# Bias tables written head by head, and the first norm's sums taken from rows of the input by ScalarE

## The chip, the cores and the metric

The kernel runs on one NeuronCore of a Trainium2 chip, as one launch. The metric is the device time of that launch in microseconds (us). TensorE's granted clock stands in the profile as a share of its upper level: 1.00 is 2.4 GHz, 0.50 is 1.2 GHz.

## The reference

One decoder layer on x of 512 rows (tokens) and 2048 columns, all in float32. What matters here:

```python
h = rmsnorm(x, norm_pre_g)                     # x * rsqrt(mean(x*x over 2048 columns) + 1e-6) * g
proj = h @ w_in                                # one projection for everything below
# group A: differential attention, 8 heads; logits + T5 relative bias, causal softmax
# group B: 8 heads over a shared latent (ckv); an indexer (iq, ik, iw) picks 128 keys for each query;
#          logits + T5 relative bias
y = concat(o_a * silu(za), o_b * silu(zb)) @ w_out
x = x + rmsnorm(y, norm_post_g)
```

The bias of a head depends only on the distance of query and key, so one row of 512 numbers for each of the 16 heads holds all of it.

## The kernel before

**Projections.** Everything is kept transposed, tokens along the free axis. The input comes twice: `xT`, 16 tiles of 128 columns by 512 tokens, which the products need, and `xn`, the rows, which before were read only at the end for the residual. Each matmul in float32 is split in a high and a low part (`hh`, `hl` of the input, `wh`, `wl` of a weight) and done as three products (`triple`, L162 to L164). The weights come in *units* of up to 128x1024 in the order in which they are used: units 0 to 5 for ckv (`wck`), 6 and 7 for the indexer's keys (`wik`), and from unit 8 on two to a projection of 128 outputs (`wT`): gate, iq, gate, iq and so on. A unit is loaded by SP's queue into `wf` (2 buffers), then split by ScalarE (`wh`, L124) and VectorE (`wl`, L125) into 3 buffers; `use` asks for that some units ahead.

**The first norm's scale.** The projections are made from x times g, without the row scale; the scale comes in when a projection leaves PSUM, as a multiplication by `rB`. Before, GpSimd squared each tile of `xT` (L185) and TensorE summed the squares over the 128 partitions by four products with a column of ones, `ssx` (L195). `rstd` (L203, L204) makes the reciprocal root `rx`, GpSimd lays it on the diagonal of `dg` (L210) and one product with `ones` (L211, `spread`) brings it to all partitions; ScalarE copies it to `rB` (L219). Projections leave PSUM through three `pj` banks, and none can leave before `rB` is there.

**The bias.** A product (L327) makes the bias rows of 16 heads, VectorE copies them (L330), and GpSimd's queue writes them to DRAM (`bd`, L332). `lay_tables` (L341) then writes each row 128 times into a DRAM table, each time one element further, so that a plain read (`strip`, L347, SP's queue) gives the 128x512 tile of biases which a head needs.

**What sets the order.** The code is handed to a scheduler that places the instructions of each engine; each engine, and SP's queue of DMA starts, then takes its own in the order placed. An instruction that waits holds up all behind it on that engine. `strip` has two buffers, and the scheduler has placed the reads for heads 0 and 1 early in SP's queue, among the weight loads.

Of the kernel before, what the change touches and what calls it, by code (L numbers as in the profile page):

```python
# [5 lines left out]
F32 = mybir.dt.float32  # L6
F32R = mybir.dt.float32r
AF = mybir.ActivationFunctionType
OP = mybir.AluOpType
# [4 lines left out]
D = 2048  # L14
KT = 16
# [10 lines left out]
def hybrid_layer(tc, xT, xn, wck, wT, wik, wva, wuv, wo, gpre, gpost, sub, kvg, ikg, lq1, lk1, lq2, lk2, relb, oneh, out):  # L26
    nc = tc.nc
    from contextlib import ExitStack
    with ExitStack() as st:
        S = st.enter_context(tc.tile_pool(name="s", bufs=1))  # L30
        P = st.enter_context(tc.tile_pool(name="p", bufs=1, space=PSUM))
        DR = st.enter_context(tc.tile_pool(name="d", bufs=1, space=DRAM))
# [4 lines left out]
        def lg_bank():  # L37
            return P.tile([128, 512], F32, name="lg", bufs=2)
# [7 lines left out]
        def tmp(name="tq", bufs=2):  # L46
            return S.tile([128, 512], F32, name=name, bufs=bufs)
# [42 lines left out]
        def load_to(n):  # L90
            while pos["load"] < min(n, len(units)):
                i = pos["load"]
                ap, shp = units[i]
                c = shp[0] * shp[1]
                nm, bf = ("wf", 2) if flags["begin"] is not None else ("qk", 4)
                t = S.tile([128, 1024], F32, name=nm, bufs=bf)
                with tc.high_priority(lead()):
                    nc.sync.dma_start(t[:, :c], ap)
                stage[i] = t
                pos["load"] += 1  # L100
# [3 lines left out]
        def split_to(n):  # L104
            while pos["split"] < min(n, len(units)):
                i = pos["split"]
                load_to(i + 1)
                c = units[i][1][0] * units[i][1][1]
                t = stage.pop(i)
                names = [("wh", 3), ("wl", 3)]  # L110
                if i >= len(units) - 8:
                    names = [last.pop(0), last.pop(0)]
                w = []
                for nm, bf in names:
                    if nm == "pt0a":
                        w.append([S.tile([128, 512], F32R, name=x, bufs=1) for x in ("pt0a", "pt0b")])
                    else:
                        a = S.tile([128, 1024], F32R, name=nm, bufs=bf)
                        w.append([a[:, :512], a[:, 512:]] if units[i][1][1] == 512 else [a[:, :c]])
                m = c // len(w[0])  # L120
                with tc.high_priority(lead()):
                    for q in range(len(w[0])):
                        src = t[:, q * m:(q + 1) * m]
                        nc.scalar.copy(w[0][q], src)  # L124
                        nc.vector.tensor_tensor(w[1][q], src, w[0][q].bitcast(F32), op=OP.subtract)  # L125
                ready[i] = w
                pos["split"] += 1

        def use(ahead=3):
            i = pos["use"]  # L130
            pos["use"] += 1
            if ahead:
                load_to(i + ahead + 1)
                split_to(i + ahead)
            nk, n = units[i][1]
            w = ready.pop(i)
            per = nk // len(w[0])
            return [[w[a][k // per][:, (k % per) * n:(k % per + 1) * n] for k in range(nk)] for a in range(2)]
# [11 lines left out]
        onec = S.tile([128, 1], F32, name="onec")  # L150
# [2 lines left out]
        nc.gpsimd.memset(ones, 1.0)  # L153
        ident = S.tile([128, 128], F32, name="ident")
        make_identity(nc, ident)
        ssx = P.tile([128, 4], F32, name="av", bufs=1)
        gp = S.tile([128, KT], F32, name="gp")
        xts, hh, hl, sqx = [], [], [], []
        ckp = [lg_bank(), lg_bank()]

        def triple(ps, a, b, x, y, k):
            nc.tensor.matmul(ps, a, x, start=(k == 0), stop=False)  # L162
            nc.tensor.matmul(ps, a, y, start=False, stop=False)  # L163
            nc.tensor.matmul(ps, b, x, start=False, stop=(k == KT - 1))  # L164

        for n, (ka, kb) in enumerate(CUTS):
            for k in range(ka, kb):
                t = S.tile([128, 512], F32, name=f"go{k}")
                nc.sync.dma_start(t, xT[k])
                xts.append(t)  # L170
                if k == 0:
                    nc.sync.dma_start(gp, gpre)
                    load_to(1)
                if k + 1 < KT and k + 1 == kb - 1:
                    load_to(n + 2)
            for k in range(ka, kb):
                a = S.tile([128, 512], F32R, name=f"hh{k}")
                b = S.tile([128, 512], F32R, name=f"hl{k}")
                nc.scalar.activation(a, xts[k], AF.Copy, scale=gp[:, k:k + 1])
                nc.vector.scalar_tensor_tensor(b, xts[k], gp[:, k:k + 1], a.bitcast(F32),  # L180
                                               op0=OP.mult, op1=OP.subtract)
                hh.append(a)
                hl.append(b)
                sq = S.tile([128, 512], F32, name="tq", bufs=2)
                nc.gpsimd.tensor_tensor(sq, xts[k], xts[k], op=OP.mult)  # L185
                sqx.append(sq)
            split_to(n + 1)
            wh, wl = use(0)
            for k in range(ka, kb):
                for u in range(2):  # L190
                    cs = slice(u * 128, u * 128 + 128)
                    triple(ckp[u], wh[k - ka][:, cs], wl[k - ka][:, cs], hh[k], hl[k], k)
                sq = sqx[k]
                for i in range(4):
                    nc.tensor.matmul(ssx[:, i:i + 1], sq[:, i * 128:(i + 1) * 128], onec,  # L195
                                     start=(k == 0 and i == 0), stop=(k == KT - 1 and i == 3))
        flags["begin"] = tc.cur_priority

        mhalf = S.tile([128, 4], F32, name="mhalf")
# [2 lines left out]
        def rstd(dst, ssq, n):  # L202
            nc.vector.tensor_scalar(dst, ssq, 1.0 / n, EPS, op0=OP.mult, op1=OP.add)  # L203
            nc.gpsimd.tensor_tensor(dst, dst, mhalf[:, :dst.shape[1]], op=OP.pow)  # L204
# [6 lines left out]
            nc.tensor.matmul(bank, ones, dg, start=True, stop=True)  # L211


        rx = S.tile([128, 4], F32, name="rx")
        rstd(rx, ssx, D)
        rB = S.tile([128, 512], F32, name="rB")
        bank = av_bank()
        spread(rx, bank)
# [8 lines left out]
        def proj_T(n0=0, m=128):  # L227
            ps = proj_bank()
            kk = 0
            while kk < KT:  # L230
                wh, wl = use()
                for a, b in zip(wh, wl):
                    triple(ps[:m, n0:], a, b, hh[kk][:, n0:], hl[kk][:, n0:], kk)
                    kk += 1
            return ps

        def pair(name, bufs):
            return S.tile([128, 2, 512], F32R, name=name, bufs=bufs)
# [25 lines left out]
        def scaled(ps, scale, n0=0):  # L264
            t = tmp()
            nc.vector.scalar_tensor_tensor(t[:, n0:], ps[:, n0:], scale, rB[:, n0:], op0=OP.mult, op1=OP.mult)  # L266
            return t
# [4 lines left out]
        for u in range(2):  # L272
            t = S.tile([128, 512], F32, name="e", bufs=2)
# [3 lines left out]
        for u in range(2):  # L277
            sq = tmp()
# [20 lines left out]
        sq = tmp()  # L299
# [31 lines left out]
        bd = DR.tile([16, 640], F32, name="bd")  # L331
# [2 lines left out]


        W = 768
        tables = [DR.tile([2, 128, W], F32, name=f"table{n}") for n in range(8)]

        def lay_tables(n):
            d = tables[n]  # L340
            nc.gpsimd.dma_start(bass.AP(tensor=d.tensor, offset=d.offset, ap=[[128 * W, 2], [W + 1, 128], [1, 640]]),  # L341
                                bass.AP(tensor=bd.tensor, offset=bd.offset + 2 * n * 640,
                                        ap=[[640, 2], [0, 128], [1, 640]]))

        def strip(h):
            g = S.tile([128, 512], F32, name="strip", bufs=2)
            nc.sync.dma_start(g, tables[h // 2][h % 2, :, 127:639])  # L347
            return g


# [16 lines left out]
        def gate():  # L367
            m = len(go)
            ps = proj_T()
            t = tmp()  # L370
            nc.vector.tensor_tensor(t, ps, rB, op=OP.mult)
            g = S.tile([128, 512], F32, name=f"go{m}")
            nc.scalar.activation(g, t, AF.Silu)
            go.append(g)
            if m < 8:
                lay_tables(m)


        def select():
# [17 lines left out]
        for m in range(8):  # L397
            ps = proj_T(n0=128)
            t = scaled(ps, 1.0, 128)
            iq = pair("v", 3)  # L400
            stacked(iq, t, 128)
            for i in range(1, 4):
# [3 lines left out]
                for g in range(2):  # L406
                    h = 2 * m + g
# [155 lines left out]
        for h in range(8):  # L563
# [3 lines left out]
            t = scaled(proj_T(), 0.125)  # L567
            q = pair("qk", 4)
            stacked(q, t)
            t = scaled(proj_T(), 1.0)  # L570
            k = pair("qk", 4)
# [33 lines left out]
        for n in range(4):  # L605
# [30 lines left out]
            for i in range(4):  # L636
# [12 lines left out]
                for a, b in zip(cuts, cuts[1:]):  # L649
                    o = (banks[i] if a == 0 else proj_bank())[:, a:b]  # L650
                    for kp in range(8):
# [3 lines left out]
                        for k in range(2):  # L655
# [5 lines left out]
                                             stop=(kk == 15))  # L661
# [7 lines left out]
                for q in range(4):  # L669
                    if i == 3 and q == 1:  # L670
                        t = S.tile([128, 512], F32, name="sq", bufs=1)
# [72 lines left out]
```

## Time and profile before

| | |
|---|---|
| runs | 1090.49, 1091.66, 1092.74 us; median 1091.66 |
| the profiled execution | 1091.52 us; span 1089.7 us from first to last instruction |
| TensorE busy | 1064.5 us |
| TensorE, mean granted clock | 0.990 |
| VectorE, ScalarE, GpSimd busy | 573.3, 411.9, 90.8 us |
| DMA | 111.97 MB, mean 103 GB/s |

TensorE is busy nearly throughout, so a time saved anywhere else shows only where TensorE waits for it. The span leaves out 1.8 us of the profiled execution's own time.

### The profile page before, as it was taken

The page shows a single profiled execution, that of the slowest core. Times are in us where ns is not written, and L with a number is a line of the kernel's source. Part 1 is how long each engine was busy: PE and PEld are TensorE (multiplying, and loading weights), DVE is VectorE, ACT ScalarE, POOL GpSimd, SP SyncE. Part 2 cuts the span into 40 slices and gives each one's busy share as a digit, 9 for nine tenths or more (in the row PEclk, how much of TensorE's full clock was granted, in tenths as well). Part 3 has the DMA queues.
Part 4 walks back from the last instruction along what each step waited for, and adds up shares of the span by engine and source line. Part 5 has one row for each costly group of instructions (what it writes and reads, how often), then busy time and mean ns, then how long its engine had stood idle before and what let it go on. Part 6 is the DMA issues. An engine that isn't in the chain of part 4 may idle for free.

```text
span 1089.7 us, 14175 instructions
## 1 busy us (share of the span) xinstructions
PE 1064.5 (98%) x5531; PEld 914.8 (84%) x5531; DVE 573.3 (53%) x1143; ACT 411.9 (38%) x773; POOL 90.8 (8%) x110
## 2 busy tenths in 40 slices
PE   8999949999999999999999999999999999999997
PEld 6888848898889889889889888888888888888886
DVE  7225526457993456456456457554545565423353
ACT  6124324333222356356356356332323353323320
POOL 4323300000000001101101100200000000000001
PEclk9999969999999999999999999999999999999999
DMA  8122572222232232222222223222222232333445
GB/s 280 59 93 82 143 210 97 97 97 93 82 100 94 97 97 78 85 90 81 88 84 86 88 71 105 88 86 79 87 68 88 87 97 79 98 108 105 136 134 193
DMA packets 43154, 111.97 MB, mean 103 GB/s; under 512 B 11504, under 2 KB 11632, under 8 KB 43088
## 3 DMA queue, kind: packets, MB, share of 16 engines
q1 hardware_dynamic: 34128, 104.49, 29.3%
q0 software_dynamic: 8960, 6.59, 2.6%
q8 instruction: 43, 0.70, 0.3%
q14 instruction: 23, 0.19, 0.1%
HBM read 106.77 MB, written 9.48 MB: 107 GB/s over the span
## 4 chain that ended last, share of the span: by engine, by line
PE 93%; DMA 4%; issue 2%; SPq 0%; POOL 0%; ACT 0%; DVE 0%; DVEq 0%; ACTq 0%; POOLq 0%
PE pj L162 18%; PE pj L163 18%; PE pj L164 18%; PE pj L461 3%; PE pj L460 3%; PE pj L459 3%; PE lg L544 3%; PE av L442 3%; PE pj L616 2%; PE pj L618 2%; PE pj L617 2%; DMA table<-bd 2%; PE tr L431 2%; PE lg L260 2%; PE lg L262 2%
## 5 line engine op out<-in xcount | busy, mean ns | idle before, releaser
L164 PE MATMUL pj<-hh,wl 128*128 128x512 f32 (+2 forms) x912 | 353.7, 388 | 0.0
L162 PE MATMUL pj<-hh,wh 128*128 128x512 f32 (+2 forms) x912 | 352.2, 386 | 0.1
L163 PE MATMUL pj<-hl,wh 128*128 128x512 f32 (+2 forms) x912 | 351.0, 385 | 0.0
L124 ACT CAST wh<-wf 128x1024 fp32r<-128x1024 f32 (+2 forms) x181 | 164.7, 923 | 428.5 <-PE pj L163 205.2
L125 DVE TENSOR_TENSOR wl<-wf,wh 128x1024 fp32r<-128x1024 f32 (+2 forms) x181 | 191.8, 1071 | 233.7 <-ACT wh L124 230.9
L164 PEld LDWEIGHTS pj<-hh,wl 128*128 128x128 f32 (+1 forms) x912 | 171.3, 188 | 31.8 <-issue 1.8
L162 PEld LDWEIGHTS pj<-hh,wh 128*128 128x128 f32 (+1 forms) x912 | 171.4, 188 | 31.4 <-issue 1.7
L163 PEld LDWEIGHTS pj<-hl,wh 128*128 128x128 f32 (+1 forms) x912 | 171.2, 188 | 30.8 <-issue 0.7
L461 PE MATMUL pj<-wh,hl 128*128 128x256 f32 x256 | 74.4, 291 | 0.0
L459 PE MATMUL pj<-wh,hh 128*128 128x256 f32 x256 | 73.1, 286 | 0.0
L460 PE MATMUL pj<-wl,hh 128*128 128x256 f32 x256 | 72.7, 284 | 0.0
L266 DVE SCALAR_TENSOR_TENSOR tq<-pj,rB 128x512 f32<-128x512 f32 (+1 forms) x40 | 26.6, 664 | 64.3 <-PE pj L164 63.5
L459 PEld LDWEIGHTS pj<-wh,hh 128*128 128x128 f32 x256 | 48.8, 191 | 1.1 <-issue 0.7
L461 PEld LDWEIGHTS pj<-wh,hl 128*128 128x128 f32 x256 | 48.9, 191 | 0.8 <-issue 0.7
L460 PEld LDWEIGHTS pj<-wl,hh 128*128 128x128 f32 x256 | 48.9, 191 | 0.4
L204 POOL TENSOR_TENSOR ro<-ro,mhalf 128x4 f32<-128x4 f32 x8 | 9.6, 1201 | 400.9 <-DVE ro L203 400.9
L544 PE MATMUL lg<-ck,qk 128*128 128x256 f32 (+3 forms) x192 | 38.3, 325 | 0.0
L617 PE MATMUL pj<-wl,hh 128*128 128x512 f32 x96 | 37.5, 391 | 0.0
L616 PE MATMUL pj<-wh,hh 128*128 128x512 f32 x96 | 37.3, 391 | 0.0
L618 PE MATMUL pj<-wh,hl 128*128 128x512 f32 x96 | 37.2, 389 | 0.0
L544 PEld LDWEIGHTS lg<-ck,qk 128*128 128x128 f32 x192 | 31.9, 189 | 3.6 <-issue 0.2
L413 DVE SCALAR_TENSOR_TENSOR sc<-e,iw,sc 128x256 f32<-128x256 f32 (+2 forms) x45 | 27.7, 616 | 10.1 <-ACT e L409 8.0
(349 smaller groups left out, 1514.3 us busy)
## 6 DMA issues: line engine op xcount, KB each, us to landing
wf<-in_wT_dram SPq DMA_DIRECT2D x112, 512.0 KB, 3.5
wf<-in_wo_dram SPq DMA_DIRECT2D x32, 512.0 KB, 3.5
wf<-in_wva_dram SPq DMA_DIRECT2D x16, 512.0 KB, 3.5
table<-bd POOLq DMA_DIRECT2D x8, 640.0 KB, 20.5
go<-in_xT_dram SPq DMA_DIRECT2D x16, 256.0 KB, 6.0
strip<-table SPq DMA_DIRECT2D x16, 256.0 KB, 3.5
out_dram<-go SPq DMA_DIRECT2D x16, 256.0 KB, 3.7
e<-in_xn_dram SPq DMA_DIRECT2D x8, 256.0 KB, 3.4
```

What stands on the lines that cost most here:

```text
L124: nc.scalar.copy(w[0][q], src)
L125: nc.vector.tensor_tensor(w[1][q], src, w[0][q].bitcast(F32), op=OP.subtract)
L162: nc.tensor.matmul(ps, a, x, start=(k == 0), stop=False)
L163: nc.tensor.matmul(ps, a, y, start=False, stop=False)
L164: nc.tensor.matmul(ps, b, x, start=False, stop=(k == KT - 1))
L459: nc.tensor.matmul(o, hh[kk][:, ts], wh[k], start=(kk == 0 and i % 2 == 0), stop=False)
L460: nc.tensor.matmul(o, hh[kk][:, ts], wl[k], start=False, stop=False)
L461: nc.tensor.matmul(o, hl[kk][:, ts], wh[k], start=False, stop=(kk == 15 and i % 2 == 1))
L544: nc.tensor.matmul(bank[:, :w], q[u][:, x, i * 128:(i + 1) * 128], ck[u][:, y, :w], start=(n == 0), stop=(n == 5))
L616: nc.tensor.matmul(banks[i], oh_[kk][:, ts], wh[k], start=(kk == 0), stop=False)
L617: nc.tensor.matmul(banks[i], oh_[kk][:, ts], wl[k], start=False, stop=False)
L618: nc.tensor.matmul(banks[i], ol_[kk][:, ts], wh[k], start=False, stop=(kk == 15))
```

## The change

It touches two things. First, GpSimd's squares and the products with the column of ones are dropped; in their place SP's queue loads the rows of x in eight pieces of 128x1024 into `v` (three buffers), ScalarE squares each and sums along the row, and VectorE adds the two halves. Second, the eight table writes of two heads each, made at the gates, become sixteen of one head each, made where the head's strip is read; the tables get a common name with two buffers.

```diff
-        ssx = P.tile([128, 4], F32, name="av", bufs=1)
...
-                sq = S.tile([128, 512], F32, name="tq", bufs=2)
-                nc.gpsimd.tensor_tensor(sq, xts[k], xts[k], op=OP.mult)
-                sqx.append(sq)
...
-                sq = sqx[k]
-                for i in range(4):
-                    nc.tensor.matmul(ssx[:, i:i + 1], sq[:, i * 128:(i + 1) * 128], onec,
-                                     start=(k == 0 and i == 0), stop=(k == KT - 1 and i == 3))
...
+        ssx = S.tile([128, 8], F32, name="ssx")
+        for i in range(4):
+            for hf in range(2):
+                t = S.tile([128, 1024], F32, name="v", bufs=3)
+                nc.sync.dma_start(t, xn[i * 128:(i + 1) * 128, hf * 1024:(hf + 1) * 1024])
+                nc.scalar.activation(t, t, AF.Square, accum_out=ssx[:, hf * 4 + i:hf * 4 + i + 1])
         rx = S.tile([128, 4], F32, name="rx")
-        rstd(rx, ssx, D)
+        nc.vector.tensor_tensor(rx, ssx[:, 0:4], ssx[:, 4:8], op=OP.add)
+        rstd(rx, rx, D)
...
         W = 768
-        tables = [DR.tile([2, 128, W], F32, name=f"table{n}") for n in range(8)]
-
-        def lay_tables(n):
-            d = tables[n]
-            nc.gpsimd.dma_start(bass.AP(tensor=d.tensor, offset=d.offset, ap=[[128 * W, 2], [W + 1, 128], [1, 640]]),
-                                bass.AP(tensor=bd.tensor, offset=bd.offset + 2 * n * 640,
-                                        ap=[[640, 2], [0, 128], [1, 640]]))
 
         def strip(h):
+            d = DR.tile([128, W], F32, name="table", bufs=2)
+            nc.gpsimd.dma_start(bass.AP(tensor=d.tensor, offset=d.offset, ap=[[W + 1, 128], [1, 640]]),
+                                bass.AP(tensor=bd.tensor, offset=bd.offset + h * 640, ap=[[0, 128], [1, 640]]))
             g = S.tile([128, 512], F32, name="strip", bufs=2)
-            nc.sync.dma_start(g, tables[h // 2][h % 2, :, 127:639])
+            nc.sync.dma_start(g, d[:, 127:639])
             return g
...
-            if m < 8:
-                lay_tables(m)
```

On TensorE, where `rx` is spread (the product `av<-dg,ones`, in the middle of the first iq projection, `pj` of 384 columns), the order before was:

```order
L162 MATMUL pj<-hh_295,wh 128x384
L163 MATMUL pj<-hl_296,wh 128x384
L164 MATMUL pj<-hh_295,wl 128x384
L211 MATMUL av<-dg,ones 128x512 [waits DVE_49,Pool_49]
L162 MATMUL pj<-hh_345,wh 128x384
```

and is now:

```order
L162 MATMUL pj<-hl_145,wh 128x384
L163 MATMUL pj<-hh_144,wl 128x384
L161 MATMUL pj<-hh_148,wh 128x384
L203 MATMUL av<-dg,ones 128x512 [waits PE_49,Pool_49]
L162 MATMUL pj<-hl_149,wh 128x384
```

Before, 36 of this projection's 48 products stood ahead of it; now 13 do.

SP's queue, from the last tile of `xT` on (`go15`), with the buffer numbers kept; `wf` are weight units 7, 8, 9, 10, 11, and `v` the pieces of x. Now:

```order
L168 DMA go15_270<-in_xT_dram 128x512 [waits DMAHW7_49]
L98 DMA wf_399<-in_wik_dram 128x640 [waits DMAHW0_49]
L98 DMA wf_401<-in_wT_dram 128x1024 [waits DMAHW1_49]
L210 DMA v_319<-in_xn_dram 128x1024 [waits DMAHW2_49]
...
L98 DMA wf_403<-in_wT_dram 128x1024 [waits DMAHW5_49,DMAHW0_49,DVE_49]
L210 DMA v_328<-in_xn_dram 128x1024 [waits DMAHW6_49,Activation_49]
...
L98 DMA wf_441<-in_wT_dram 128x1024 [waits DMAHW1_49,DVE_49]
L210 DMA v_337<-in_xn_dram 128x1024 [waits DMAHW2_49,Activation_49]
L98 DMA wf_531<-in_wT_dram 128x1024 [waits DMAHW5_49,DMAHW3_49,DVE_49]
L210 DMA v_340<-in_xn_dram 128x1024 [waits DMAHW4_49,Activation_49]
```

Before, the weight units followed each other here. From the fourth piece on, a load waits for ScalarE to have squared the piece three before it.

GpSimd's queue where the tables are written, with buffer numbers, before (the first three of eight) and now (the first three of sixteen, which follow each other without anything between them):

```order
L332 DMA bd_583<-v_580 16x640 [waits DMASW1_49,DVE_49]
L341 DMA table0_585<-bd_583 2x128x640 [waits DMASW2_49,DMASW1_49]
L341 DMA table1_586<-bd_583 2x128x640 [waits DMASW3_49]
L341 DMA table2_587<-bd_583 2x128x640 [waits DMASW4_49]
```

```order
L331 DMA bd_512<-v_509 16x640 [waits DMASW1_49,DVE_49]
L339 DMA table_2869<-bd_512 128x640 [waits DMASW2_49,DMASW1_49]
L339 DMA table_3162<-bd_512 128x640 [waits DMASW3_49]
L339 DMA table_3691<-bd_512 128x640 [waits DMASW4_49]
```

Each write has a table of its own, and none waits for a strip to be read, only for GpSimd's own earlier DMAs (DMASW). The writes stay at the same place in GpSimd's queue; each now has 128 rows as its outer dimension, where before it had 2. SP's queue reads the strips of heads 0 and 1 after the same sixteen loads of `wT` as before; the second now waits for a table of its own.

## Rows read from the trace of the kernel before

**Rows 1.** The page's first part: busy time, share of the span, instructions.
```profile
PE 1064.5 (98%) x5531; PEld 914.8 (84%) x5531; DVE 573.3 (53%) x1143; ACT 411.9 (38%) x773; POOL 90.8 (8%) x110
```

**Rows 2.** Waits of TensorE: total, times, longest (us).
```profile
PE lg L260 <- ACT e L409: 13.9, 1, 13.9
```

**Rows 3.** Chain that ended last, start: start, length (us), what.
```profile
20.26 0.79 PE av L195 x8
21.05 0.35 PE lg L163
...
39.04 1.68 PE av L195 x16
40.72 0.30 PE pj L162
41.03 0.23 PE pj L163
...
52.21 1.68 PE av L195 x16
```

**Rows 4.** The line L195, its instructions: duration min/median/max (ns), first and last start.
```profile
L195 PE MATMUL av<-onec,tq x128: 164/250/250, 16.5 to 66.0; 128*128 128x1 f32 x128
```

**Rows 5.** Windows: length, busy PE, PEld, DVE, ACT, POOL, clock, DMA share, GB/s.
```profile
20.00:30.00 10.00, 10.00 (x62) 8.77 (x61) 10.00 (x16) 6.21 (x9) 4.80 (x4) 1.00 0.55 214
```

**Rows 6.** Timeline, ScalarE, GpSimd and TensorE up to the spread: start, length (us).
```profile
30.18 0.73 ACT L124 CAST wh<-wf 128x640 fp32r<-128x640 f32 x1 [2.95 <-issue]
...
66.49 1.04 POOL L204 TENSOR_TENSOR rx<-rx,mhalf 128x4 f32<-128x4 f32 x1 [5.71 <-DVE rx L203]
67.63 3.25 POOL L210 TENSOR_SCALAR dg<-ident,rx 128x128 f32<-128x128 f32 x4
...
73.82 1.02 PE L211 MATMUL av<-dg,ones 128*128 128x512 f32 x2
```

**Rows 7.** Groups by line and shape, ScalarE: busy us, mean ns | idle before, releasers.
```profile
L124 ACT CAST wh<-wf 128x1024 fp32r<-128x1024 f32 x128 | 134.1, 1048 | 354.0 <-PE pj L163 203.7 <-issue 102.3 <-DMA wf<-in_wT_dram 21.6
```

**Rows 8.** DMA issues, whole span: count, size, median us to landing.
```profile
wf<-in_wT_dram SPq DMA_DIRECT2D x112, 512.0 KB, 3.5
...
strip<-in_gpost_dram POOLq DMA_DIRECT2D x4, 256.0 KB, 4.1
```

**Rows 9.** Waits of SP's queue: total, times, longest (us).
```profile
SPq L347 <- DMA table<-bd: 20.1, 1, 20.1
```

**Rows 10.** Timeline, GpSimd and SP's queue around the tables: start, length (us).
```profile
122.05 7.51 POOL L341 DMA_DIRECT2D table<-bd  x7 [2.13 <-DMA bd<-v]
...
140.70 1.55 SPq L347 DMA_DIRECT2D strip<-table  x2
```

**Rows 11.** DMA issues in short stretches (first table, eighth table, first weight load behind the strips).
```profile
table<-bd POOLq DMA_DIRECT2D x1, 640.0 KB, 18.6
...
table<-bd POOLq DMA_DIRECT2D x1, 640.0 KB, 21.8
...
wf<-in_wT_dram SPq DMA_DIRECT2D x1, 512.0 KB, 10.6
```

**Rows 12.** DMA queues, 100 to 185 us: packets, MB, share of 16 engines' time.
```profile
q0 software_dynamic: 8384, 5.41, 26.1%
```

**Rows 13.** Timeline, TensorE, from the bias product past the long wait.
```profile
117.38 1.03 PE L327 MATMUL tr<-pt0b,rb 32*16 32x512 f32 x2
...
140.17 0.33 PE L162 MATMUL pj<-hh,wh 128*128 128x384 f32 x1
140.34 0.34 PE L163 MATMUL pj<-hl,wh 128*128 128x384 f32 x1
154.54 0.79 PE L260 MATMUL lg<-qk,v 128*128 128x512 f32 x1 [13.86 <-ACT e L409]
...
157.37 0.52 PE L164 MATMUL pj<-hh,wl 128*128 128x384 f32 x1
...
159.61 0.42 PE L162 MATMUL pj<-hh,wh 128*128 128x384 f32 x1
```

More of the change, by code (lines that the diff above doesn't have):

```diff
@@ L155, in hybrid_layer @@
         make_identity(nc, ident)
-        ssx = P.tile([128, 4], F32, name="av", bufs=1)
         gp = S.tile([128, KT], F32, name="gp")
-        xts, hh, hl, sqx = [], [], [], []
+        xts, hh, hl = [], [], []
         ckp = [lg_bank(), lg_bank()]
```

## The prediction

> **What bounds the kernel now.** I read the busy times first, then TensorE's waits, then the chain that ended last. TensorE is busy 98% of the span [rows 1], so only two things can make the kernel faster: fewer TensorE cycles, or less waiting of TensorE. The list of waits says where the second is: the longest by far is one of 13.9 us, for ScalarE's `e` (L409) [rows 2]. The timeline puts it between 140.5 and 154.5 us, and shows a cost behind it: products of 384 columns that followed each other after 0.17 us (140.17 to 140.34) follow after 0.32 from 157.37 to 159.61 [rows 13]. That is TensorE at its lower clock level, from 154.5 to 159.6, so about half of 5.1 us is lost, 2.5 us.
>
> Where does the wait come from? SP's queue waits 20.1 us for a bias table [rows 9]. The tables are issued from 122.05 on; SP starts the two strip reads at 140.70, is through with them at 142.25, and only then starts the next weight unit [rows 10]. That one needs 10.6 us to land, beside the tables' writes [rows 11], against a median of 3.5 us [rows 8]: 152.9. ScalarE's cast of it, 1.05 us [rows 7], and the `e` behind it bring TensorE to 154.5. So the wait for a table, at the head of a queue that also feeds the weights, is the only hole in TensorE's work. The first hundred microseconds have none: between 20 and 30 us TensorE is busy 10.00 of 10.00 [rows 5].
>
> **The column products.** They are 128 records on TensorE [rows 4], 16 tiles by 4 products by 2. In the chain they stand in eight groups of x8 at 0.79 us and four of x16 at 1.68 [rows 3]: 6.3 + 6.7 = 13.0 us. Behind a group the next product takes 0.35 or 0.30 in place of 0.23 [rows 3], 8 x 0.12 + 4 x 0.07 = 1.2. Sum 14.3 us, all of it in a stretch in which TensorE waits for nothing, so I count all of it. The bound from below: VectorE is just as full from 20 to 30 us [rows 5], it makes `hl`, and a TensorE without these groups might catch up with it. Four single groups lie there; if VectorE gave none of them back, 3.6 us would be lost. Against that, its operations on the port it shares work with GpSimd's squares beside them, which go too. I take no loss, and keep the 3.6 for the range.
>
> **The row sums.** Added: eight loads of 512 KB, at 3.5 us like a weight unit [rows 8]; eight squares, nearest row the cast of the same size, 1.05 us [rows 7], 8.4 us in all on ScalarE, busy 6.21 of 10 in the fullest stretch [rows 5]; one small addition on VectorE. All of it is free as long as `rx` is there when TensorE comes to its spread, and that spread now stands 23 products of 384 columns earlier. So: before, TensorE got there at 73.82 [rows 6]; less 14.3, less 23 x 0.17 = 4.0, it gets there at 55.5. When is `dg` ready? The last two squares stand on ScalarE behind the cast of unit 10, which waits for TensorE to end the indexer's key projection. Before, that ended at 52.21, where a group of x16 follows it [rows 3]; seven single groups and two double ones lay ahead, 9.9 us, so now at 42.3. Cast and two squares, 3 x 1.05: 45.5. From there to the end of `dg` the same steps took 66.49 to 70.88, 4.4 us [rows 6]; with the addition and two hand-overs, 51. Some 4.5 us are left. The last two pieces of x are loaded when squares 4 and 5 free their buffers, about 39 to 40 us, and land at 43 to 44, in time. If each took the 10.6 us that is this trace's dear case [rows 11], the eighth square would end at 52 and TensorE wait 1 to 2 us. Price 0, bounds 0 and 2.
>
> **The tables.** The bytes are the same, 16 x 320 KB. What counts is when tables 0 and 1 have landed, since SP's queue waits for these. Before, the first one took 18.6 us, and the eighth, issued last of all, 21.8 [rows 11]; seven were issued within 7.5 us [rows 10]. First and last took about as long, so a table was slow by itself and not because of its place in the queue. All tables together need 26.1% of 85 us of all sixteen engines, 22.2 us [rows 12], 1.4 us for a head's table if it gets all of them. What does a table of the new form take? Bounds: the old 18.6 for the first and about one more for the second, and from below GpSimd's other write of similar size, 256 KB in 4.1 us [rows 8], plus 1.4. The order shows that the new write has 128 rows as its outer dimension, like that 4.1 us one, where the old had 2. I take the near end: the first at 5 us, the second at 6.5.
>
> The Trainium skill, "DMA: Bandwidth & Descriptors", section "Rules for kernel authors", speaks against this change: coalesce small transfers, since each pays some 2 us; its fit of 2.0 us plus bytes at 436 GB/s gives 3.5 us for an old table. The trace disagrees, with 18.6. By that fit the old form would have cost TensorE no wait, and splitting could gain nothing there. Another line of the same section would explain the 18.6: the slowest dimension of the pattern sets how many engines a DMA uses, so an outermost 2 confines it to 2. By this rule the new form runs on 16, and the near end is the right one.
>
> Now the clock of it, counted from the bias product at 117.38 [rows 13]. Before, tables started at +4.7 and TensorE ran dry at +23.1. In the new order 19 more products of 384 columns stand between the bias product and that place, 3.3 us, so it runs dry at +26.4. To be in time the unit must land 1.6 us ahead (152.9 to 154.5, as above), +24.8; with 10.6 to land it must be started by +14.2; with 1.55 for the two strips, table 1 must have landed by +12.7, which is 8.0 us after the tables' start. At 6.5 it is in time: no wait, and no fall of the clock. This gains 13.9 + 2.5 = 16.4. If table 1 came at t us, TensorE would wait t - 8.0. At the far end, 19.7, that is 11.7 us and a fall of the clock again: 2.2 us gained in place of 16.4.
>
> Weight units after that one have more time: the stock ahead of TensorE was worth some 20 us, as the 20.1 us block against a 13.9 us wait shows.
>
> **The sum.** 1091.5 (profiled execution; the median of the runs is 1091.7, so the two may stand for each other) - 14.3 - 13.9 - 2.5 = 1060.8. I say **1061**.
>
> **Rivals.**
> *Tables late in part.* Eight writes in flight share the engines packet by packet, and table 1 lands with the others, near 8 x 1.4 = 11 to 12 us after the start. Wait 3 to 4 us, some of the clock's 2.5: 1065 to 1067. For it: before, the first of seven in flight was not served first.
> *Tables as late as before.* The size of the write, not its form, was slow: wait 11.7, clock 2.5, so 1075. For it: no table of the new form is in the trace. The skill's rule on coalescing, above, points this way.
> *Start fed too slowly.* VectorE or the x loads hold TensorE by 2 to 5 us before 56 us, at the spread or ahead of it: 1063 to 1066.
> *The homes don't take turns.* The words of the change speak of two; the order shows sixteen tables without a wait on a strip. If turns were kept, a write would wait for a read made a whole head earlier, and cost nothing: 1061 again.
> *Slower than before: the pieces of x come singly.* If three buffers did not overlap and each of the last five pieces took 10.6 to land and 1.05 to square, one behind the other from about 30 us, where ScalarE turns to the cast ahead of the first squares [rows 6], the eighth would end at 88, `dg` at 93.5, and TensorE wait 38 us at its spread: 1099. It turns to slower where the eighth square ends 30.7 + 4.5 us after the 45.5 above, at about 81. Against it: nothing else wants the DMA engines then, and loads land in 3.5.
>
> **Numbers.** Forecast 0.66; tables late in part 0.13; as late as before 0.05; start too slow 0.11; slower 0.03; the remaining 0.02 for no change at all. The forecast's own range is 1058 to 1064 (relief of VectorE from GpSimd on one side, 3.6 lost on the other). The range to hold 8 in 10 reaches over the partial cases: **1058 to 1070**. A measurement of this kernel tells a change from none at about 0.2%, 2.2 us; the cases give faster 0.95, same 0.02, slower 0.03.
>
> **What will show it.** Right: no line with the column of ones before the ckv norm; the spread of `rx` near 55 us without a wait of TensorE ahead of it; SP's wait for tables of some 5 us instead of 20.1; the first tables landing in 4 to 7 us; no wait of 13.9 and a granted clock of 1.00 from 130 to 170 us; everything from there 30 us earlier. Wrong: a TensorE wait ahead of the spread, released by GpSimd; tables that still land after 15 us or more; weight units that land in over 12 us while the tables are written, so that a shorter hole stays.

## The result and the profile after

The changed kernel took 1062.15 us (median of 4 runs, 1061.28 to 1062.52), the kernel before 1091.81 (4 runs): a ratio of 0.9728, 95% interval [0.9711, 0.9745]. That is 29.7 us faster, 1.15 us above the forecast. The profiled execution took 1062.16 us, its span 1060.1, at a mean granted clock of 0.997.

**Where the time went.** The page's first part, to be held against [rows 1]:

```profile
PE 1048.4 (99%) x5403; PEld 898.0 (85%) x5403; DVE 568.0 (54%) x1144; ACT 420.9 (40%) x789; POOL 69.5 (7%) x102
```

The span fell by 29.6 us, from 1089.7. TensorE is busy 16.1 us less and idle 13.5 us less: two nearly equal halves, one of work that is gone (and of the lower clock behind the old wait), one of waiting. Its waits that are left:

```profile
PE lg L161 <- ACT wh L124: 1.3, 1, 1.3
PE av L149 <- DVE mhalf L192: 1.2, 1, 1.2
PE lg L161 <- ACT hh L178: 0.8, 1, 0.8
PE lg L162 <- DVE hl L179: 0.3, 1, 0.3
```

All four are in the first 20 us. No line waits for an `e`, where [rows 2] had 13.9. In the list of waits of SP's queue the table costs 3.3 us in two waits, against 20.1 [rows 9]:

```profile
SPq L342 <- DMA table<-bd: 3.3, 2, 2.3
```

The timeline of the changed kernel at the two places of the prediction (start, length in us; in brackets the idle time ahead of it and its releaser):

```profile
46.50 1.06 ACT L211 ACTIVATE v<-v 128x1024 f32<-128x1024 f32 x1 [0.89 <-DMA v<-in_xn_dram]
47.47 0.18 ACT L211 ACTIVATION_READ_ACCUMULATOR v<-v 128x1 f32 x1
...
48.14 1.04 POOL L196 TENSOR_TENSOR rx<-rx,mhalf 128x4 f32<-128x4 f32 x1 [40.95 <-DVE rx L195]
49.28 3.09 POOL L202 TENSOR_SCALAR dg<-ident,rx 128x128 f32<-128x128 f32 x4
...
56.70 1.02 PE L203 MATMUL av<-dg,ones 128*128 128x512 f32 x2
...
100.37 1.03 PE L326 MATMUL tr<-pt0b,rb 32*16 32x512 f32 x2
...
105.93 4.21 POOL L339 DMA_DIRECT2D table<-bd  x8 [2.64 <-DMA bd<-v]
...
110.61 1.73 SPq L342 DMA_DIRECT2D strip<-table  x2
113.11 18.47 SPq L98 DMA_DIRECT2D wf<-in_wT_dram  x4
...
126.35 0.59 ACT L402 ACTIVATE e<-lg 128x512 f32<-128x512 f32 x1
...
127.84 0.28 PE L259 MATMUL lg<-qk,v 128*128 128x256 f32 x1
```

The upper half is the first norm: the eighth square ends at 47.5, `dg` is ready at 52.4, TensorE spreads it at 56.70 without a wait, 4.3 us later. The lower half is the tables: issued from 105.93, and 4.7 us later SP reads the first strip, where it was 18.7 before [rows 10]. The DMA issues in short stretches (the first two tables; the first weight unit behind the strips; the pieces of x from 14 to 45 us) and the queue of the table writes over 85 us, 78 to 163:

```profile
table<-bd POOLq DMA_DIRECT2D x2, 320.0 KB, 5.1
...
wf<-in_wT_dram SPq DMA_DIRECT2D x1, 512.0 KB, 12.2
...
v<-in_xn_dram SPq DMA_DIRECT2D x8, 512.0 KB, 5.1
...
q0 software_dynamic: 1344, 5.35, 19.1%
```

The same bytes as in [rows 12] now go in 1344 packets in place of 8384. And busy times by stretch (length, PE, PEld, DVE, ACT, POOL, clock, DMA share, GB/s):

```profile
20.00:25.00 5.00, 5.00 (x23) 4.11 (x22) 4.97 (x10) 4.49 (x8) 0.00 (x0) 1.00 1.01 382
...
105.00:125.00 20.00, 20.00 (x100) 17.68 (x99) 10.01 (x14) 6.70 (x11) 8.39 (x16) 1.00 0.90 291
125.00:145.00 20.00, 20.00 (x103) 17.98 (x102) 11.73 (x16) 9.42 (x16) 0.00 (x0) 1.00 0.53 183
```

TensorE is busy without a gap, at a granted clock of 1.00 (the 2.4 GHz level), all through the writing of the tables. But the reserve is small. The weight unit behind the strips was started at 113.11 and took 12.2 us: it landed 24.9 us after the bias product, and by the prediction's count it was needed at 24.8. The `e` that ScalarE makes behind its cast ended at 126.94, and TensorE came for it at 127.84: 0.9 us to spare.

### The profile page after: what moved, and what is told of

It is laid out like the page before. It is cut to its first block, busy times and chain, and to the rows that moved or that the text cites. A ratio compares the mean times of both kernels' runs of the same rounds, so it can differ in the third digit from the quotient of the medians.

```text
span 1060.1 us, 13936 instructions
## 1 busy us (share of the span) xinstructions
PE 1048.4 (99%) x5403; PEld 898.0 (85%) x5403; DVE 568.0 (54%) x1144; ACT 420.9 (40%) x789; POOL 69.5 (7%) x102
## 3 DMA queue, kind: packets, MB, share of 16 engines
q1 hardware_dynamic: 35280, 108.68, 31.4%
## 4 chain that ended last, share of the span: by engine, by line
PE 97%; DMA 1%; SPq 1%; DVE 0%; issue 0%; ACT 0%; DVEq 0%; POOL 0%; ACTq 0%; POOLq 0%
PE pj L162 19%; PE pj L163 19%; PE pj L161 19%; PE pj L454 3%; PE pj L453 3%; PE pj L452 3%; PE lg L537 3%; PE av L435 3%; PE pj L609 2%; PE pj L611 2%; PE pj L610 2%; PE lg L259 2%; PE lg L261 2%; PE tr L424 2%; PE lg L611 1%; PE lg L610 1%
```

## The experiments

Theory: the column products and the wait for the tables are two separate gains, of 14.3 and 16.4 us; a table came late because of the form of its write, an outermost dimension of 2. Rivals: the size of the write; the order of instructions that came along with the change; relief of VectorE from GpSimd's squares. All ratios are to the kernel before, timed beside each kernel (medians 1091.3 to 1091.9).

**norm_only**: the changed norm with the eight old table writes.

```diff
-            nc.gpsimd.dma_start(bass.AP(tensor=d.tensor, offset=d.offset, ap=[[W + 1, 128], [1, 640]]), ...
+            nc.gpsimd.dma_start(bass.AP(tensor=d.tensor, offset=d.offset, ap=[[128 * W, 2], [W + 1, 128], [1, 640]]), ...   # at the gates, lay_tables(m)
```

> The changed kernel with the eight table writes of before (two heads each, outermost dimension 2). Theory: the two parts gain apart, 14.3 us of TensorE work and 16.4 us of one wait with the clock behind it. The write keeps its 18.6 us, so SP's queue waits for it and TensorE runs dry again, though later in its order than before: a wait of 7 to 12 us, clock at its lower level for some 5 us behind it, 1071 to 1076 us. Rival 1, the earlier start of everything ends the wait by itself: 1062. Rival 2, the column products were hidden and all the gain is the tables': 1088 or more.

Measured: 1071.62 us, ratio 0.9818 [0.9803, 0.9833], 20.0 faster. Its list of waits, TensorE and then SP's queue:

```profile
PE lg L259 <- ACT e L408: 7.8, 1, 7.8
```

```profile
SPq L346 <- DMA table<-bd: 17.2, 1, 17.2
```

The wait for `e` is back, but at 7.8 us in place of 13.9: 14.3 of products plus 6.1 of wait make 20.4. The tables are as slow as before; TensorE only has more work placed ahead of the hole: it runs dry 31.4 us after the bias product (101.39 to 132.80), where it was 23.3.

**tables_only**: the kernel before with the sixteen new writes.

```diff
+            d = DR.tile([128, W], F32, name="table", bufs=2)
+            nc.gpsimd.dma_start(... ap=[[W + 1, 128], [1, 640]] ...)   # in strip(h), in place of lay_tables(m)
```

> The kernel before with the sixteen table writes of one head each (outermost dimension 128); the column products stay. Theory: first table in 4 to 5 us, second about 6 us after the start. In the order of before TensorE runs dry 3.3 us sooner after the bias product than in the changed kernel, whose unit came just in time, so a wait of 2.5 to 3.5 us stays: 1078 to 1080 us. Rival, the parts simply add up: 1075. Rival, the tables were not the cause: 1091.

Measured: 1081.66 us, 0.9914 [0.9898, 0.9929], 10.0 faster and not 16.4. TensorE's waits:

```profile
PE lg L260 <- ACT e L403: 3.5, 1, 3.5
PE lg L162 <- ACT wh L124: 2.4, 2, 1.9
PE lg L162 <- ACT hh L179: 1.4, 1, 1.4
```

The strip is read 5.5 us after the first table's issue (124.98 to 130.47), yet 3.5 us of the wait remain: the products that the change moved ahead of the hole are missing here, so that TensorE comes to the place 23.3 us after the bias product, against 27.5 in the changed kernel, and the weight unit behind the strips takes 13.1 us to land. So the moved products were part of the second gain, not only the tables. The wait is 3.5 of the 6.4 us that are missing. Another 2.8 were lost ahead of the bias product, which stands at 120.20 in place of 117.38 [rows 13], with the same instructions in the same order up to there; what made them is open.

**pairs_rows_out**: the changed kernel with eight writes of two heads (640 KB), 128 rows outermost.

```diff
-  ap=[[W + 1, 128], [1, 640]]
+  ap=[[W + 1, 128], [128 * W, 2], [1, 640]]      # eight, at the gates
```

> The changed kernel with eight writes of two heads each, 640 KB as before, but with the 128 rows as the outermost dimension and the two heads inside. Form theory (the outermost 2 made the write slow): the first pair lands in about 6 us, no long wait of TensorE, 1062 us, within 2. Size theory (two heads in a write made it slow): the pair takes 18 us, and the time is that of the changed norm with the old tables, 1071 to 1076.

Measured: 1061.02 us, 0.9719 [0.9703, 0.9735], the changed kernel's time. The timeline of it, GpSimd and SP:

```profile
108.02 5.48 POOL L340 DMA_DIRECT2D table<-bd  x8 [2.58 <-DMA bd<-v]
...
113.41 0.94 SPq L346 DMA_DIRECT2D strip<-table  x2
```

The old size, and the strip is read 5.4 us after the first issue. The size of the write was not what made it slow; writing head by head was not needed. Nor was it the order of instructions: pairs_rows_out and norm_only run the same instructions in the same order on every engine, and differ in the pattern of the eight writes alone, 1061.02 against 1071.62.

**before_rows_out**: the kernel before, nothing else but the two dimensions exchanged.

```diff
-  ap=[[128 * W, 2], [W + 1, 128], [1, 640]]
+  ap=[[W + 1, 128], [128 * W, 2], [1, 640]]
```

> The kernel before with nothing changed but the order of two dimensions in the table write, 128 rows outermost, two heads inside. Form theory: the first pair lands in about 6 us, TensorE's wait of 13.9 us falls to 0 to 3.5, 1075 to 1080 us. Size theory: the write is as slow as before, 1091.

Measured: 1084.06 us, 0.9927 [0.9912, 0.9942], 4 us over the expected range, though the first table landed in 5.6 us and the strip was read after 5.7. DMA issues of the first table and of the weight unit behind the strips, and TensorE's longest wait:

```profile
table<-bd POOLq DMA_DIRECT2D x1, 640.0 KB, 5.6
...
wf<-in_wT_dram SPq DMA_DIRECT2D x1, 512.0 KB, 14.4
```

```profile
PE lg L260 <- ACT e L409: 4.2, 1, 4.2
```

Three things make the miss. The unit behind the strips took 14.4 us where it had taken 10.6 [rows 11]. While the unit was in flight, the queue of the table writes took a larger share of the engines' time: first here, from 131.6 to 146 us, then in the kernel before, from 142.4 to 153:

```profile
q0 software_dynamic: 742, 3.37, 75.2%
```

```profile
q0 software_dynamic: 3209, 1.22, 63.8%
```

The wait of 4.2 follows from the late unit (131.58 + 14.4 + 1.6 = 147.58, where TensorE goes on). Behind that wait the clock falls as before (0.90 between 145 and 180 us), so its 2.5 us are not gained. And the bias product stands at 120.08 in place of 117.38 [rows 13], 2.7 us lost in the first 25 us, although every instruction up to there is the same, in the same order. Executions of one kernel can differ by as much: the profiled one of pairs_rows_out took 1064.22 us, its bias product at 102.52, and its three others 1060.90 to 1061.08. Whether that is the cause here is not shown. 1091.5 - 13.9 + 4.2 + 2.7 = 1084.5 is the time of it.

**head_outer2, head_outer2_again, head_outer8**: sixteen writes of one head, 320 KB as in the changed kernel, with the 128 rows cut in 2 x 64 or in 8 x 16.

```diff
-  ap=[[W + 1, 128], [1, 640]]
+  ap=[[W + 1, 2], [2 * (W + 1), 64], [1, 640]]     # head_outer2
+  ap=[[W + 1, 8], [8 * (W + 1), 16], [1, 640]]     # head_outer8
```

> The changed kernel, one head to a write, 320 KB, but the 128 rows written as odd and even rows, so that the outermost dimension is 2. Form theory: half the bytes of the old write at the old pace, 9 to 10 us to land, table 1 some 10 us after the start in place of 6; the weight unit behind it, which came just in time, comes 4 us late, with some lower clock: 1065 to 1069 us. Size theory: as the changed kernel, 4.7 us to land, 1062.

> head_outer2 once more, for a profile: the profiled execution of the first run took 3323 us, with TensorE three times slower throughout. Expected as then in its other executions: 1064 to 1067, a TensorE wait of 1.5 to 6 us for an e after the bias product, tables 0 and 1 landing in 8 to 12 us. If the slow TensorE belongs to the kernel, it shows again; if it was an accident of one execution, it doesn't.

> As the run with an outermost 2, with 8 in its place. Form theory, if the pace goes with the outermost dimension: about a quarter of the time of an outermost 2 for the data, 3 to 5 us to land, 1062 to 1063 us. If any split of the rows costs as much as the 2: 1065 to 1069.

Measured: head_outer2 1065.11 us (the median without one execution of 3323 us, see the end), 0.9764 [0.9744, 0.9784]; again 1066.74, 0.9765 [0.9736, 0.9795]; head_outer8 1061.55, 0.9725 [0.9711, 0.974]. head_outer2_again, timeline, queue and wait:

```profile
105.98 6.42 POOL L339 DMA_DIRECT2D table<-bd  x8 [2.59 <-DMA bd<-v]
...
116.54 1.72 SPq L342 DMA_DIRECT2D strip<-table  x2
```

```profile
q0 software_dynamic: 8512, 5.41, 25.9%
```

```profile
PE lg L259 <- ACT e L402: 2.0, 1, 2.0
```

With 2 outermost the strip is read after 10.6 us, with 8 after 4.9 (106.06 to 111.00), with 128 after 4.7; the instructions around them are the same, in the same order. The 2 also brings back the small packets and the share of [rows 12]: 8512 packets in the same 85 us, where head_outer8 has 2368. So the outermost dimension sets the pace, 8 is already enough, and the hole opens again when table 1 comes late enough: it landed 11.9 us after the tables' start, for which the prediction's t - 8.0 gives a wait of 3.9 us, and 2.0 came.

The trace also keeps sixteen landing marks for each DMA. Of the first table of the kernel before, fourteen stand within 4.1 us of the issue and the last two at 17.8 and 18.6. Of head_outer2_again's, fourteen stand within 2.7 us and two at 10.5; of head_outer8's, eight within 1.8 us and eight from 4.2 to 4.9; of the changed kernel's, all sixteen from 2.9 to 4.7.

The Trainium skill, "DMA: Bandwidth & Descriptors", section "Why a DMA increments its semaphore by 16 and not by 1", says that a DMA uses as many engines, up to 16, as divide its slowest dimension. The marks agree: two late ones with a 2, eight with an 8, sixteen together with 128. That 8 engines do here nearly what 16 do, 4.9 us against 4.7, is no contradiction, with eight writes in flight. The fit of the same page, 2.0 us plus bytes at 436 GB/s, which stands in "Anatomy of one DMA — SWDGE (gpsimd) path" and not in "Rules for kernel authors", has no term for this: it gives 3.5 us for the 640 KB that took 18.6 and 5.6.

**x_single**: the pieces of x go through one buffer.

```diff
-                t = S.tile([128, 1024], F32, name="v", bufs=3)
+                t = S.tile([128, 1024], F32, name="ck0", bufs=1)
```

> The changed kernel with one buffer for the pieces of x in place of three, so that each load waits for the square before it. Theory: each piece takes 3.5 to 5 us to land, 1.25 to square and about 0.5 to hand over, and waits now and then behind a cast; the eighth square ends near 70 to 76 us in place of 47, so the spread of the row scale, which had some 4 us to spare and now stands behind 35 more products, waits 12 to 18 us, with the clock at its lower level behind it: 1075 to 1083 us. Rival, the row sums have time to spare anyway: 1062.

Measured: 1081.98 us, 0.991 [0.9893, 0.9927], 20 slower than the changed kernel. TensorE's waits:

```profile
PE av L203 <- POOL dg L202: 9.3, 1, 9.3
PE lg L259 <- ACT e L402: 3.4, 1, 3.4
PE av L282 <- ACT tq L278: 2.1, 1, 2.1
```

The squares come 4 to 7 us apart, the last ends at 66.9 in place of 47.5, and TensorE waits 9.3 us at the spread. The mechanism of the prediction's slow rival is real. Its price, 38 us, was made with 10.6 us a load; the loads took 4.1.

**both_sums**: the changed kernel with GpSimd's squares and the column products put back, their sums used by nothing.

```diff
+                sq = S.tile([128, 512], F32, name="tq", bufs=2)
+                nc.gpsimd.tensor_tensor(sq, xts[k], xts[k], op=OP.mult)
...
+                    nc.tensor.matmul(ssc[:, i:i + 1], sq[:, i * 128:(i + 1) * 128], onec, ...)
```

> The changed kernel with GpSimd's squares and the column products put back beside the row sums; their result is not used. Theory: the products are pure TensorE time on the path, 14.3 us more than the changed kernel, 1076 us, within 2. Rival, the gain came from the shorter chain to the row scale and not from TensorE's time: 1062 to 1065.

Measured: 1076.72 us, 0.9863 [0.9846, 0.9879], 14.6 above the changed kernel. Products and squares together cost 14.6; counted were 14.3. TensorE's waits, besides the 1.2 us of its first instruction:

```profile
PE lg L162 <- ACT wh L124: 1.9, 1, 1.9
PE lg L164 <- DVE wl L125: 1.3, 1, 1.3
PE lg L267 <- ACT e L410: 0.6, 1, 0.6
```

**keep_squares**: of these, the squares alone.

> The changed kernel with GpSimd's sixteen squares of the input's tiles put back, their results used by nothing; no column products. Before, the squares ran beside VectorE's making of the low parts at the start. Theory A: the gain of the first norm is TensorE's column products alone, so the time stays that of the changed kernel, 1062 us (1061 to 1063). Theory B: GpSimd's squares slowed VectorE at a port that they share, and part of the 14 us was VectorE's relief: 1064 to 1067, with a TensorE wait on hl before 45 us and longer mean durations of hl in the trace.

Measured: 1068.55 us, 0.9781 [0.9758, 0.9803], 6.4 above the changed kernel. So with the squares left in, taking out the products is worth 8.2 us, and taking out the squares as well another 6.4, though they are on GpSimd, which is busy 9% of the time here. The split holds for this order of taking out alone: with the products in place, in both_sums, the squares cost TensorE no wait for `hl`. VectorE's lines from 12 to 45 us, by shape, in keep_squares and then in the changed kernel:

```profile
L179 DVE SCALAR_TENSOR_TENSOR hl<-go,gp,hh 128x512 fp32r<-128x512 f32 x13 | 14.5, 1153 | 0.0
L125 DVE TENSOR_TENSOR wl<-qk,wh 128x768 fp32r<-128x768 f32 x3 | 6.3, 2101 | 0.0
```

```profile
L179 DVE SCALAR_TENSOR_TENSOR hl<-go,gp,hh 128x512 fp32r<-128x512 f32 x12 | 8.6, 746 | 3.6 <-ACT hh L178 3.6
L125 DVE TENSOR_TENSOR wl<-qk,wh 128x768 fp32r<-128x768 f32 x2 | 1.9, 958 | 0.3 <-ACT wh L124 0.3
```

The same operation takes 1153 ns in place of 746, the wide one 2101 in place of 958. What that does in a stretch, and to TensorE's waits:

```profile
20.00:25.00 5.00, 3.25 (x13) 2.10 (x12) 5.00 (x4) 4.45 (x7) 5.00 (x4) 1.00 1.04 410
```

```profile
PE lg L162 <- DVE hl L179: 3.9, 4, 1.5
PE lg L161 <- ACT wh L124: 2.5, 2, 1.4
PE lg L163 <- DVE wl L125: 1.6, 1, 1.6
```

VectorE and GpSimd are both full, VectorE ends 4 operations where it ended 10, and TensorE is busy 3.25 of 5. Without the column products TensorE asks for `hl` sooner, and nothing paces the squares, which before had to wait for the products to free `tq` (22.4 us of GpSimd's idle time in the kernel before). The Trainium skill, "SBUF — State Buffer", section "SBUF: two separate sides", says that a VectorE operation with two SBUF inputs and a GpSimd operation that reads SBUF lock each other out for a whole instruction. The trace agrees: 2101 - 958 = 1.14 us is about the length of one square, 1.03 to 1.75 us here.

**x_on_pool**: the pieces of x issued from GpSimd's queue.

```diff
-                nc.sync.dma_start(t, xn[...])
+                nc.gpsimd.dma_start(t, xn[...])
```

> The changed kernel with the eight loads of x's rows issued from GpSimd's queue in place of SP's. Theory A: the 1.2 us that the changed kernel lost at its start come from SP's queue, whose order of xT tiles and weight units changed when the pieces of x joined it; with the pieces elsewhere the first weight unit lands near 14.3 us again and the time is 1060 to 1061. Theory B: the start is set by the DMA engines, filled by about 10 us of transfers in any order, and the change in order does not matter: 1062, the first product no earlier. If the pieces, now free to start at once, take the engines from the xT tiles and first weights, it is slower: 1063 to 1067.

Measured: 1076.07 us, 0.9852 [0.9828, 0.9876], 14 slower than the changed kernel; theory A and theory B both fail, and it is beyond the 1063 to 1067 of the third case. TensorE's waits:

```profile
PE lg L161 <- ACT wh L124: 7.4, 2, 5.1
PE lg L259 <- ACT e L402: 5.2, 1, 5.2
```

The pieces start at once and stand in the way of the first weights (384 KB units land in 12.7 us), as the expectation's last sentence had it, and the granted clock falls to 0.59 between 15 and 20 us. What it had not foreseen: with the pieces out of SP's queue the scheduler places the strip reads two weight units earlier, SP waits 8.1 us for tables, and the hole at `e` opens again. On SP's queue the pieces wait their turn behind the weights, and by this run that is what keeps them cheap.

## Why the prediction was right

Forecast 1061.0, measured 1062.15. By its steps:

- **Column products, 14.3**: 14.6 by both_sums. The size was right, the reason only in part. The prediction took the products' own time as the gain and kept 3.6 us for a VectorE that might not keep up, with the relief from GpSimd's squares against it. keep_squares shows that the relief was needed: had the squares stayed, 6.4 of the 14.6 us would not have come.
- **The wait of 13.9 and the clock's 2.5**: the wait is gone and the clock is 1.00 in the stretch. TensorE's busy time fell by 16.1, where 14.3 + 2.5 = 16.8 were counted.
- **Tables at 5 and 6.5 us**: 4.7 and 6.0 after the tables' start. The cause, the outermost dimension, is shown by pairs_rows_out, which clears the size and, against norm_only, the order, and by head_outer2, which restores the delay.
- **The unit behind the strips, 10.6**: mis-sized, it took 12.2, and 13.1 and 14.4 in tables_only and before_rows_out. One of the prediction's own signs of being wrong, over 12 us, came, without the hole that was to go with it. The unit started as counted, 12.7 us after the bias product, and the extra 1.6 us would have used up the 1.5 that 6.5 against 8.0 left in hand. A second slip made up for it: the count of the moved work has 19 products of 384 columns, 3.3 us, and leaves out four of 512, 0.9 us. TensorE came to the place 27.5 us after the bias product and not 26.4, and 0.9 us were left. That the two slips cancel is luck.
- **A stock of some 20 us ahead of later units** does not follow from its two numbers: a block of 20.1 us and a landing 7.1 us longer, against a wait of 13.9, leave some 13. Nothing in the sum hangs on it.
- **`dg` at 51, spread at 55.5**: 52.4 and 56.7. The loads took 5.1 us in place of 3.5, and each square has an accumulator read of 0.18 behind it; TensorE was 1.2 us late itself, so 4.3 of the 4.5 us were left.
- **The 1.2 us that are missing** are in the first 20 us. Up to `dg` the spread was to come 18.3 us earlier and came 17.1 (73.82 to 56.70). That the new order of SP's queue costs this is not shown: between the profiled executions of the kernel before and of before_rows_out the very same order differs by 2.7 us at the bias product.

Of the rivals, "tables late in part" is what head_outer2 did, "start fed too slowly" what keep_squares and x_on_pool did, and the single pieces what x_single did; in the changed kernel none did. tables_only waited with its tables in time, for want of the moved products. By the rival of the homes nothing was lost: each wait of a table's issue has an earlier table write as its releaser. Apart, the two halves of the change gained 20.0 and 10.0 us; made together, they gained 29.7. That is not 14.3 and 16.4: each half already shortens the one wait, norm_only by 6.1 us with its moved products and tables_only by 10.4 with its earlier tables. That the sum fits so well is partly chance, since 2.8 us of tables_only's gain were lost at its start.

No run beats the changed kernel by more than its uncertainty: pairs_rows_out (0.9719) and head_outer8 (0.9725) stand with it (0.9728).

## What to carry to other kernels

When a small DRAM write is slow, read the order of its dimensions before its size: 128, or 8, outermost in place of 2 made the same 640 or 320 KB land two to three and a half times sooner. An engine that is busy 9% of the time can still cost TensorE 6 us if it works beside the full one that feeds TensorE: price the removal of such work by what it shares. And once a wait is gone, count again what arrives next; here the next load came with 0.9 us to spare, and six of the ten other kernels waited 2 us or more for `e`.

## What the runs showed of the hardware that was not expected

- The packets of a DRAM write depend on the form of its pattern too: 8384 and 8512 in 85 us with 2 outermost, 2368 with 8, 1344 with 128, for the same 5.4 MB. GpSimd's time to issue one goes with it: 0.80, 0.60 and 0.52 us for one head.
- Faster tables mostly made the weight load behind the strips slower: 10.1 to 10.7 us with 2 outermost (three kernels), 10.7 to 14.4 with the 128 rows outermost (eight kernels, 12.2 in the changed one). With 8 outermost it took 9.0.
- With the same instructions in the same order, the first 25 us vary by 2 to 3 us between profiled executions (bias product at 117.38 before, 120.08 and 120.20 in before_rows_out and tables_only; 100.37 in the changed kernel, 102.52 in pairs_rows_out).
- One execution of head_outer2, the profiled one, took 3323 us. Its three-term products took 1007 ns in the mean, against 388 in head_outer2_again, at a granted clock that the record shows as 1.00, while VectorE, ScalarE and GpSimd were as busy as ever. The seven other executions of the same code took 1064.8 to 1068.0. What it was stays open.
